# A planner's allowance for late operands of the tensor engine, applied only behind the in-projection

## Chip, cores and metric

The kernel runs on one core of a Trainium2 chip. The metric is the device time of one execution in microseconds (us). Engines are named as in the profile: PE is the tensor engine, DVE the vector engine, ACT the scalar engine, POOL GpSimd, and SP SyncE, which here issues every DMA.

## What is computed

One decoder layer on 1024 tokens of width 1024, all in float32. Two head groups, eight heads each, read one normed input through one input projection; their outputs go through one output projection, and a SwiGLU feed-forward part follows.

```python
xn = rms_norm(x, norm1_g)
proj = xn @ w_in                                  # 1024 x 3328
q, k, v, p_rw = split(proj, [512, 1024, 1536])
attn = rms_norm(dilated_attention(q, k, v))       # three dilated windows, ALiBi
rwkv = rwkv7_time_mix(p_rw, ...)                  # a scan over the tokens, 64 x 64 state per head
x = x + concat([attn, rwkv]) @ w_out
xn2 = rms_norm(x, norm2_g)
out = x + (silu(xn2 @ w_gate) * (xn2 @ w_up)) @ w_down
```

## The kernel before

Every wide product is made of three matmuls on operands split into a high and a low part: one block of 1024 x 128 weights takes 24 matmuls of 512 columns for each half of the tokens. The program has four stretches.

1. The in-projection (`inproj`, weights from `fetches` and `load_in`, results taken by `feed`): 26 blocks of 128 columns in `blocks`, the recurrence's first, then q, k and v. Each block is done for both halves of the tokens.
2. The recurrence (`decays`, `keys`, `scoring`, `sides`, `turn`, `invert`, `merge`, `chain`, `post`) runs beside it. There are eight units (four pairs of heads, two halves of the tokens) of eight steps each; 64 steps must follow one another. `chain` is the sequential part; each step goes back and forth between PE and the copying engines:

```python
yield PE.matmul(out=X[:, 0:128], lhsT=ra[:, c, :], rhs=Sc, ...)          # "S,ra"
for o in halves:
    yield DVE.tensor_copy(R[o, o], X[64:128, o])
yield PE.matmul(out=X[:, 128:256], lhsT=M[:, 1, c, :], rhs=R, ...)       # "Rb,M"
yield DVE.tensor_copy(vs[64:128, :], X[64:128, 128:256])
for o in halves:
    yield ACT.activation(Uc[o, o], X[64:128, 128 + o.start:128 + o.stop], AF.Copy)
yield PE.matmul(out=X[:, 256:384], lhsT=kbT[:, c, :], rhs=vs, ...)       # "VS,kbT"
yield PE.matmul(out=X[:, 0:128], lhsT=M[:, 1, c, :], rhs=Uc, ...)        # "Ub,M"
for e in range(2):
    yield DVE.scalar_tensor_tensor(out=Sn[o, o], ...)                    # state of the next step
```

   `post` norms a unit's output and stores it to `mix_d`.
3. Attention (`attn_load`, `value_load`, `attend` with `near` and `far`, `finish`) and the output projection (`fetch_wo`, `load_wo`, `mix_load`, `mix_T`, `outproj`, `add_up`). Attention's pool `pa` is opened when the in-projection is through; the output projection's pool lies where the recurrence's tiles were, and its streams are added when the recurrence is through.
4. The feed-forward part (`fetch_ff`, `prepare_ff`, `ffproj`, `gates`, `hidden`, `weight_sums`, `down`, `finals`).

The order of the instructions on each engine is not written out. Each part is a generator, a stream, that yields operations, waits for marks and requests for banks of PSUM. `Flow.run` keeps a clock for each engine and takes, again and again, the stream whose next operation can start first by its own costs (`scan`), by rank among those that are ready. `Flow.ready` gives the time at which an operation can start: for an operand that another engine wrote, the end of that operation plus that engine's `LAG`. For an operation of PE it adds another 60 ns and `LATE`, 300 ns. So a matmul is placed no earlier than that, and others, those of the in-projection above all, are placed ahead of it. These times only set the order; on the chip each engine runs its instructions in that order, and semaphores make it wait for real.

`flow.run` is called in turn for `dense` (the in-projection and `feed`), `rwkv` (the recurrence), `attn`, `ph3` (output projection and second norm) and the feed-forward part. All instructions are issued from one line, L235 (`emit`), so the profile's groups are told apart by their tiles: `mm`, `bank` and `chain` are banks of PSUM, `inhi` and `inlo` a block of in-projection weights, `xn0..` and `xn1..` the normed input, `kk`, `qv`, `vv` keys, queries and values of attention, `sb` its scores, `woraw`, `woh` and `wol` weights of the output projection.

Of the kernel before, what the change touches and what calls it, by code (L numbers as in the profile page):

```python
# [47 lines left out]
LAG = {"PE": 200, "ACT": 145, "DVE": 140, "POOL": 65, "SP": 1500}  # L48


LATE, SWITCH = 300, 100
# [7 lines left out]
class Op:  # L59


    def __init__(self, eng, name, fn, a, k):
        self.eng, self.name, self.fn, self.a, self.k = eng, name, fn, a, k
# [40 lines left out]
class Flow:  # L104
# [2 lines left out]


    def __init__(self):
        self.now, self.clk, self.marks, self.streams = 0.0, {}, {}, []  # L110
        self.slots, self.keys, self.count, self.shared = {}, {}, {}, set()
        self.free, self.weights, self.whole = {}, 0.0, True
# [67 lines left out]
    def ready(self, s):  # L180
        op = s.head
        if isinstance(op, Wait):
            if any(m not in self.marks for m in op.marks):
                return None
            return max((self.marks[m] for m in op.marks), default=0.0)
        if isinstance(op, Get):
            t, n = sorted(self.free[op.kind].values()), op.n or 1
            return t[n - 1] if len(t) >= n else None
        r = self.clk.get(op.eng, 0.0)
        if op.eng == "SP":  # L190
            r = max(r, self.clk.get("queues", 0.0) - 3000)
        for keys, which in ((op.rd, 0), (op.wr, 0), (op.wr, 1)):
            for k in keys:
                if k in self.slots:
                    for e, t in self.slots[k][which].items():
                        if e != op.eng or (e == "SP" and (keys is op.rd or which)):
                            r = max(r, t + LAG[e] + (60 + LATE if op.eng == "PE" else 0))
                        elif keys is op.rd and which == 0:
                            r = max(r, t + OWN[e])
        return r  # L200
# [67 lines left out]
def hymba_kernel(ctx: ExitStack, tc: tile.TileContext, x, w_in, w2a2, g2, w_out, w_gate, w_up,  # L268
# [3 lines left out]
    flow = Flow()  # L272
    ACT, DVE, POOL = Lane("ACT", nc.scalar), Lane("DVE", nc.vector), Lane("POOL", nc.gpsimd)
    PE, SP = Lane("PE", nc.tensor), Lane("SP", nc.sync)
# [1073 lines left out]


    flow.run(dense)  # L1350
    pw.__exit__(None, None, None)
    p1.__exit__(None, None, None)
    flow.free["bank"].update(mm0=flow.now, mm1=flow.now)
# [617 lines left out]
```

## Time and profile before

| what | us |
|---|---|
| median of 3 runs (lowest to highest) | 1462.24 (1461.12 to 1463.45) |
| the profiled execution's own time | 1464.17 |
| its span, first to last instruction | 1462.4 |
| PE busy in the span | 1389.5 (95%), 8578 records |
| weight loads of PE | 1123.4 (77%) |
| DVE busy | 899.8 (62%) |
| ACT busy | 726.3 (50%) |
| POOL busy | 701.4 (48%) |

The profile page gives busy time by engine, and one digit of busy share for each fortieth of the span. A matmul of float32 in two passes leaves two records. Matmuls are pipelined and their ends are modelled, so records overlap: the distance from one start to the next is the price of a matmul, not its duration. The views used below are the busy time in chosen stretches, the timeline of single engines, the list of waits, and the chain of work that ended last. In a timeline a row is a start, a duration, the engine, the operation and its tiles (written, then read), the shape, how many equal instructions it merges, and in brackets the idle time before it with what ended it.

### The profile page before, as it was taken

The page shows a single profiled execution, that of the slowest core. Times are in us where ns is not written, and L with a number is a line of the kernel's source. Part 1 is how long each engine was busy: PE and PEld are TensorE (multiplying, and loading weights), DVE is VectorE, ACT ScalarE, POOL GpSimd, SP SyncE. Part 2 cuts the span into 40 slices and gives each one's busy share as a digit, 9 for nine tenths or more (in the row PEclk, how much of TensorE's full clock was granted, in tenths as well). Part 3 has the DMA queues.
Part 4 walks back from the last instruction along what each step waited for, and adds up shares of the span by engine and source line. Part 5 has one row for each costly group of instructions (what it writes and reads, how often), then busy time and mean ns, then how long its engine had stood idle before and what let it go on. Part 6 is the DMA issues. An engine that isn't in the chain of part 4 may idle for free. (4 is left out here: it accounts for less than half of the span.)

```text
span 1462.4 us, 24926 instructions
## 1 busy us (share of the span) xinstructions
PE 1389.5 (95%) x8578; PEld 1123.4 (77%) x8578; DVE 899.8 (62%) x1812; ACT 726.3 (50%) x1794; POOL 701.4 (48%) x685
## 2 busy tenths in 40 slices
PE   7999989999999996699999899999999999999998
PEld 5777767777777885588878678888888888888887
DVE  5556677657576436667876855555555555666655
ACT  6434456566766776556764623333333333444443
POOL 4443344345565461433353845555555555644443
PEclk9999999999999998799999899999999999999999
DMA  5343222323333336699722235444444445865765
GB/s 193 115 119 72 68 80 83 94 75 110 93 110 109 110 127 175 186 280 235 198 76 75 72 115 165 151 148 146 154 151 165 153 165 181 280 200 188 225 221 173
DMA packets 217794, 213.45 MB, mean 146 GB/s; under 512 B 41026, under 2 KB 152898, under 8 KB 217667
## 3 DMA queue, kind: packets, MB, share of 16 engines
q1 hardware_dynamic: 217666, 211.85, 47.3%
q8 instruction: 68, 1.11, 0.3%
q14 instruction: 60, 0.48, 0.1%
HBM read 148.61 MB, written 58.98 MB: 142 GB/s over the span
## 5 line engine op out<-in xcount | busy, mean ns | idle before, releaser
L235 POOL TENSOR_TENSOR opl<-fraw,oph 128x512 fp32r<-128x512 f32 x79 | 110.8, 1405 | 180.7 <-PE bank L235 46.6
L235 POOL TENSOR_TENSOR opl<-raw,oph 128x512 fp32r<-128x512 f32 x74 | 97.1, 1312 | 99.9 <-ACT oph L235 95.6
L235 DVE TENSOR_TENSOR opl<-raw,oph 128x512 fp32r<-128x512 f32 x74 | 102.0, 1381 | 68.5 <-ACT oph L235 68.4
L235 ACT ACTIVATE oph<-raw 128x512 fp32r<-128x512 f32 x148 | 85.5, 624 | 114.3 <-PE mm L235 62.9
L235 ACT ACTIVATE oph<-sw 128x512 fp32r<-128x512 f32 x80 | 50.6, 633 | 180.4 <-PE chain L235 53.3
L235 POOL TENSOR_TENSOR inlo<-inraw,inhi 128x512 fp32r<-128x512 f32 x62 | 82.0, 1323 | 85.2 <-ACT inhi L235 72.7
L235 ACT ACTIVATE oph<-fraw 128x512 fp32r<-128x512 f32 x82 | 51.2, 627 | 76.7 <-PE bank L235 32.4
L235 DVE TENSOR_TENSOR opl<-sw,oph 128x512 fp32r<-128x512 f32 x80 | 75.8, 947 | 19.6 <-ACT oph L235 18.3
L235 PE MATMUL bank<-oph 128*128 128x512 f32 x154 | 59.9, 389 | 0.0
L235 PE MATMUL bank<-opl,oph 128*128 128x512 f32 x154 | 59.9, 389 | 0.0
L235 PE MATMUL bank<-oph,opl 128*128 128x512 f32 x154 | 59.9, 389 | 0.0
L235 DVE TENSOR_TENSOR uu<-bank,uu 128x512 f32<-128x512 f32 x20 | 13.9, 693 | 73.1 <-PE bank L235 73.1
L235 DVE SCALAR_TENSOR_TENSOR S<-chain,ec,Sp 64x64 f32<-64x64 f32 x112 | 31.6, 282 | 42.2 <-PE chain L235 35.5
L235 ACT ACTIVATE Ub<-chain 64x64 f32<-64x64 f32 x128 | 28.1, 219 | 54.2 <-DVE VS L235 51.9
L235 POOL TENSOR_TENSOR sw<-fraw 128x512 f32<-128x512 f32 x40 | 51.9, 1298 | 0.0
L235 ACT ACTIVATE Y<-chain 64x64 f32<-64x64 f32 x128 | 26.8, 211 | 49.0 <-DVE S L235 43.7
L235 ACT ACTIVATE inhi<-inraw 128x512 fp32r<-128x512 f32 x62 | 38.7, 624 | 16.0 <-PE mm L235 6.5
L235 DVE COPY Rb<-chain 64x64 f32<-64x64 f32 x128 | 28.9, 226 | 27.9 <-PE chain L235 25.5
L235 ACT ACTIVATE sb<-sb,mx 128x256 f32<-128x256 f32 (+3 forms) x64 | 36.2, 567 | 16.9 <-DVE mx L235 16.8
L235 POOL TENSOR_TENSOR rsf<-smf,nhalf 128x8 f32<-128x8 f32 x16 | 26.6, 1660 | 30.3 <-DVE smf L235 23.2
L235 DVE COPY VS<-chain 64x128 f32<-64x128 f32 x64 | 18.9, 295 | 31.6 <-PE chain L235 30.4
L235 PE MATMUL bank<-ra,kb 64*64 64x128 f32 x512 | 37.4, 277 | 0.0
(509 smaller groups left out, 4362.6 us busy)
## 6 DMA issues: line engine op xcount, KB each, us to landing
inraw<-in_w_in_dram SPq DMA_DIRECT2D x62, 256.0 KB, 3.0
fraw<-in_w_gate_dram SPq DMA_DIRECT2D x48, 256.0 KB, 3.8
fraw<-in_w_up_dram SPq DMA_DIRECT2D x48, 256.0 KB, 3.0
ws<-in_w_down_dram SPq DMA_DIRECT2D x22, 512.0 KB, 5.7
t_d<-ws SPq DMA_DIRECT2D x44, 256.0 KB, 3.0
raw<-s_d SPq DMA_DIRECT2D x44, 256.0 KB, 2.7
raw<-t_d SPq DMA_DIRECT2D x44, 256.0 KB, 3.1
s_d<-first SPq DMA_DIRECT2D x33, 256.0 KB, 4.1
```

What stands on the lines that cost most here:

```text
L235: op.fn(*op.a, **op.k)
```

## The change

The fixed `LATE` in `Flow.ready` becomes a field of the planner. It is 0 at first and is set to `LATE` when `flow.run(dense)` returns, that is when the planner has issued everything of the in-projection and of `feed`. Nothing else is changed; `LATE` stays 300.

```diff
     def __init__(self):
+        self.late = 0.0
         self.now, self.clk, self.marks, self.streams = 0.0, {}, {}, []
...
                     for e, t in self.slots[k][which].items():
                         if e != op.eng or (e == "SP" and (keys is op.rd or which)):
-                            r = max(r, t + LAG[e] + (60 + LATE if op.eng == "PE" else 0))
+                            r = max(r, t + LAG[e] + (60 + self.late if op.eng == "PE" else 0))
...
     flow.run(dense)
+    flow.late = LATE
     pw.__exit__(None, None, None)
```

Every engine's order changes from its first tens of instructions on. Three places follow. The first is on PE, one early step of the recurrence (the one that begins at 192.0 us in the profile), before:

```order
L235 MATMUL chain_2021<-S_118,ra 128x128
L235 MATMUL mm_2066<-xn10l,inhi 128x512 x3
L235 MATMUL mm_2066<-xn10h,inlo 128x512 x4
L235 MATMUL chain_2021<-Rb_124,M 128x128
L235 MATMUL chain_2119<-Vb_122,M 128x128
L235 MATMUL mm_2029<-xn1h_96,inhi 128x512 x2
L235 MATMUL mm_2029<-xn1h_97,inhi 128x512 x2
L235 MATMUL mm_2029<-xn1l_98,inhi 128x512 x2
L235 MATMUL mm_2029<-xn1l_99,inhi 128x512 x2
L235 MATMUL chain_2021<-VS,kbT 128x128
L235 MATMUL chain_2021<-Ub_126,M 128x128
```

The same step now:

```order
L236 MATMUL chain_1964<-S_118,ra 128x128
L236 MATMUL mm_1867<-xn11l,inhi 128x512
L236 MATMUL mm_1867<-xn11h,inlo 128x512 x4
L236 MATMUL chain_1964<-Rb_124,M 128x128
L236 MATMUL chain_2056<-Vb_122,M 128x128
L236 MATMUL mm_2050<-xn0h,inhi 128x512 x4
L236 MATMUL mm_2050<-xn0l,inhi 128x512 x2
L236 MATMUL chain_1964<-VS,kbT 128x128
L236 MATMUL chain_1964<-Ub_126,M 128x128
```

Between S,ra and Rb stand five wide matmuls instead of seven, between Rb and VS six instead of eight.

The second place is on PE, the end of the in-projection (its last block is on bank mm), before:

```order
L235 MATMUL mm_6283<-xn11h,inlo 128x512
L235 MATMUL chain_6320<-VS,kbT 128x128
L235 MATMUL chain_6320<-Ub_125,M 128x128
L235 MATMUL mm_6283<-xn11h,inlo 128x512 x2
L235 MATMUL chain_6345<-S_120,ra 128x128
L235 MATMUL chain_6345<-Rb_124,M 128x128
L235 MATMUL chain_6393<-Vb_122,M 128x128
L235 MATMUL bank_6400<-cs,vf_6398 128x128 x4
L235 MATMUL chain_6345<-VS,kbT 128x128
```

And now:

```order
L236 MATMUL mm_6475<-xn11h,inhi 128x512 x4
L236 MATMUL chain_6427<-Ub_126,M 128x128
L236 MATMUL mm_6475<-xn11l,inhi 128x512 x4
L236 MATMUL mm_6475<-xn11h,inlo 128x512 x3
L236 MATMUL bank_6526<-cs,exf_6511 128x128 x4
L236 MATMUL mm_6475<-xn11h,inlo 128x512
L236 MATMUL bank_6555<-cs,vf_6553 128x128 x4
L236 MATMUL bank_6635<-kk,qv 128x128 x2
```

Before, seven steps of the recurrence (S,ra, Rb and Ub, with six each of VS and Vb) follow the last in-projection matmul; now the last matmul of the last step, Ub_126, stands ahead of the last eight wide ones, and attention's first matmul follows the last values' transposes.

The third place is on SP, ahead of the first load of the output projection's weights, before:

```order
L235 DMA qv_6675<-qh_d_71 64x512
L235 DMA qv_6675<-ql_d_72 64x512
L235 DMA bias_6676<-in_tab_dram 128x512
L235 DMA vv_6704<-v_d_76 128x4x128
L235 DMA vv_6745<-v_d_76 128x4x128
L235 DMA mix_d_77<-Y_6318 128x2x128
L235 DMA woraw_6843<-in_w_out_dram 128x512
```

And now:

```order
L236 DMA mix_d_77<-Y_5971 128x2x128
L236 DMA v_d_76<-v01_6562 128x2x256
L236 DMA v_d_76<-v11_6563 128x2x256
L236 DMA qv_6610<-qh_d_71 64x512
L236 DMA qv_6610<-ql_d_72 64x512
L236 DMA bias_6611<-in_tab_dram 128x512
L236 DMA kk_6624<-kh_d_73 64x512 x2
L236 DMA kk_6624<-kl_d_74 64x512 x2
L236 DMA qv_6629<-qh_d_71 64x512
L236 DMA qv_6629<-ql_d_72 64x512
L236 DMA bias_6630<-in_tab_dram 128x512
L236 DMA woraw_6607<-in_w_out_dram 128x512
```

Before, the weights' load stands behind the last store of the recurrence, which comes after four heads' loads; now that store stands ahead of the last stores of the values, and the weights follow after two heads.

## Rows read from the trace of the kernel before

**Rows 1.** Busy time by stretch: us, each engine's busy us (records), clock, DMA share, GB/s.

```profile
50.00:547.00 497.00, 476.63 (x4217) 376.24 (x4215) 303.00 (x742) 299.38 (x853) 230.56 (x234) 1.00 0.33 97
547.00:561.00 14.00, 7.85 (x37) 6.28 (x35) 5.42 (x15) 8.12 (x30) 5.84 (x6) 0.68 0.56 172
561.00:596.00 35.00, 22.44 (x144) 18.08 (x143) 25.39 (x86) 18.91 (x68) 4.30 (x4) 0.98 0.44 121
596.00:623.00 27.00, 20.10 (x94) 16.06 (x95) 17.76 (x63) 17.47 (x49) 14.10 (x12) 0.70 0.95 267
623.00:761.00 138.00, 131.39 (x874) 113.78 (x873) 103.17 (x366) 93.58 (x301) 52.33 (x93) 0.99 0.76 199
761.00:802.00 41.00, 41.00 (x208) 33.98 (x207) 26.99 (x49) 19.23 (x36) 16.51 (x27) 1.00 0.30 91
842.00:1462.00 620.00, 615.44 (x2688) 503.94 (x2686) 358.74 (x411) 217.42 (x364) 326.40 (x245) 1.00 0.54 176
```

**Rows 2.** Timeline of PE, the end of the in-projection.

```profile
545.67 0.71 PE L235 MATMUL mm<-xn11h,inlo 128*128 128x512 f32 x2
546.68 0.49 PE L235 MATMUL chain<-S,ra 128*128 128x128 f32 x2 [0.29 <-DVE S L235]
...
560.49 1.84 PE L235 MATMUL bank<-kk,qv 128*128 128x128 f32 x6
```

**Rows 3.** Timeline of SP's queue, 551 to 597 us.

```profile
551.96 1.93 SPq L235 DMA_DIRECT2D v_d<-v  x2
553.98 0.45 SPq L235 DMA_DIRECT2D qv<-qh_d  x1
...
558.15 0.59 SPq L235 DMA_DIRECT2D qv<-qh_d  x1
...
595.74 0.36 SPq L235 DMA_DIRECT2D mix_d<-Y  x1
596.19 2.34 SPq L235 DMA_DIRECT2D woraw<-in_w_out_dram  x5
```

**Rows 4.** Waits of PE, 50 to 547 us: total us, times, longest.

```profile
PE chain L235 <- ACT Ub L235: 5.3, 9, 1.0
PE chain L235 <- DVE S L235: 5.1, 7, 1.8
...
PE chain L235 <- DVE Rb L235: 2.0, 5, 0.6
```

**Rows 5.** Timeline, one step of the recurrence, 419 to 424 us.

```profile
419.57 0.38 PE L235 MATMUL chain<-S,ra 128*128 128x128 f32 x2
...
419.99 0.47 DVE L235 COPY Rb<-chain 64x64 f32<-64x64 f32 x2 [0.99 <-PE chain L235]
...
420.95 0.38 PE L235 MATMUL chain<-Rb,M 128*128 128x128 f32 x2
...
421.70 0.45 ACT L235 ACTIVATE Ub<-chain 64x64 f32<-64x64 f32 x2 [0.79 <-DVE VS L235]
...
422.77 0.38 PE L235 MATMUL chain<-VS,kbT 128*128 128x128 f32 x2
...
422.99 0.39 PE L235 MATMUL chain<-Ub,M 128*128 128x128 f32 x2
```

**Rows 6.** The chain that ended last: start, us, twelve wide matmuls.

```profile
887.26 2.79 PE chain L235 x12
```

**Rows 7.** Timeline, another step of the recurrence, 196 to 198 us.

```profile
196.38 0.22 ACT L235 ACTIVATE Ub<-chain 64x64 f32<-64x64 f32 x1
...
197.22 0.49 PE L235 MATMUL chain<-VS,kbT 128*128 128x128 f32 x2 [0.85 <-ACT Ub L235]
```

**Rows 8.** Busy time from 561 to 596 us on the tiles kk, vv and sb.

```profile
561.00:596.00 35.00, 7.33 (x31) 4.86 (x30) 0.98 0.44 121
...
561.00:596.00 35.00, 6.40 (x32) 4.06 (x32) 0.98 0.44 121
...
561.00:596.00 35.00, 6.00 (x37) 4.33 (x37) 5.45 (x12) 8.57 (x25) 0.98 0.44 121
```

## Prediction

> **What bounds the kernel now.** I read the busy time by stretch first. Up to 547 us the tensor engine (PE) is busy in 476.6 of 497 us, from 623 to 802 in 172.4 of 179, and in the feed-forward part, 842 to the end, in 615.4 of 620 [rows 1]. Between 547 and 623 it is busy in only 50.4 of 76 us, and its granted clock means 0.68 and 0.70 in two of those three stretches [rows 1]. So PE work is the bound nearly everywhere, and the loose time lies behind the in-projection.
>
> The timeline says why. The last in-projection matmul starts at 545.67; behind it the recurrence still turns, with waits, and the first attention matmul comes at 560.49 [rows 2]. By the order of the instructions seven of the 60 steps with a state (those that begin with S,ra) are left then. They alternate PE, DVE and ACT, and nothing wide enough stands between. SyncE shows the other price: the last store of the recurrence (mix_d) goes out at 595.74, and the first load of the output projection's weights (woraw) only at 596.19, right behind it [rows 3].
>
> Inside the in-projection PE waits little for the recurrence: 5.3 + 5.1 + 2.0 = 12.4 us in 9 + 7 + 5 = 21 waits, out of some 165 hand-overs of these three kinds [rows 4]. There the 300 ns of allowance shows as slack: in a step that nothing hinders, the two Rb copies end at 419.99 + 0.47 = 420.46 and their matmul starts at 420.95; the Ub copies end at 421.70 + 0.45 = 422.15 and the next chain matmul starts at 422.77 [rows 5]. That is about half a microsecond to spare each time.
>
> **The change part by part.** No operation is added or removed, only the order is planned anew, with operands of PE assumed 300 ns earlier until the in-projection is through.
>
> *Work that moves.* In the new order all 64 steps stand ahead of the last in-projection matmul. 37 matmuls of 128 columns in two passes (7 each of S,ra, Rb and Ub, 6 each of VS and Vb, 4 of the gates) move from behind it to ahead of it, at 0.22 each (422.77 to 422.99 [rows 5]): 8.1 us.
>
> *Shorter cover.* Counted over the two orders at 0.23 for 512 columns (2.79 us for 12 [rows 6]) and 0.11 a record of 128 columns (half of the 0.22), the PE work between S,ra and Rb falls from a mean of 1.52 to 1.30 us, from Rb to VS from 2.28 to 1.88, from Ub to the next S,ra from 2.18 to 2.11: cuts of 0.22, 0.40 and 0.07, 0.69 a step. An unhindered step has the spare time for this [rows 5] and pays nothing. A step in which an engine's queue is late pays the whole cut: at 196.38 ACT only begins a Ub copy, and VS waits 0.85 at 197.22 [rows 7]. The 21 waits of today grow by 9 x 0.40 + 7 x 0.07 + 5 x 0.22 = 5.2 us. I take twice that, 10 us, for the hand-overs that just miss a wait today and for the others (square sums, head norms) that lose their 300 ns too. Bounds: 0, if a longer wait at one place only gives the other engines time to catch up, and 64 x 0.69 = 44, if nothing covers anything; 10 lies near the low end because the unhindered step does. So the in-projection ends at 545.67 + 0.71 + 8.1 + 10 = 564.5.
>
> *The pause.* From that end to the first load of queries (qv) pass 553.98 - 546.38 = 7.6 us [rows 2, 3]: the last values are turned, split and stored (551.96) first. This chain is not touched, and I keep 7.6; what leaves it is the recurrence, so that PE stands idle there instead. It costs nothing by itself, since before too no attention could run.
>
> *The loads.* On SyncE mix_d now stands ahead of those stores, and woraw follows after two heads' loads: ten issues. Seven took 4.17 us (553.98 to 558.15 [rows 3]), so ten take 6. Woraw goes out at 564.5 + 7.6 + 6 = 578.0 instead of 596.19: 18.2 us earlier.
>
> *Attention done before that.* What attention had done by 596 has still to be done: 31 + 32 + 37 = 100 records on the tiles kk, vv and sb [rows 8]. At the 0.11 of the smallest they are 11 us, by their busy times 7.33 + 6.40 + 6.00 = 19.7, which overlap. I take 14, nearer the low end for that overlap. From the weights' request to the end I leave the 866 us as they are: in 623 to 802 PE is all but full, and the feed-forward part is the same work.
>
> Sum: -18.2 + 14 = -4.2 us against the profiled execution's 1464.17, so 1460.0 there. It lies 1.9 above the median of the runs shown, 1462.24; against that the forecast is **1458.0 us**. A difference of 0.2%, 2.9 us, is about what a measurement can tell from none.
>
> [...] After 552 PE has no wide matmuls left, and the granted clock means 0.68 from 547 to 561; after the stall near 590 it means 0.70 from 596 to 623 [rows 1]. [...]
>
> **The rivals.**
> 1. *A larger gain.* Today attention starts with six banks and four score buffers while the recurrence holds DVE; in the new order it has eight of each from the start and the output projection at hand as filler. If the ramp of 596 to 623 goes at the pace of 623 to 761 (95% busy, clock 0.99), it gives back 27 - 20.1/0.95 = 5.8 us, and with waits of 5 instead of 10 us another 5: 1447. For it speaks the unhindered step; against it the DMA engines, 95% busy there [rows 1].
> 2. *Slower: the waits take more than the tail gives.* The place is the in-order DVE and ACT queues, where inversions, keys and norms stand ahead of the Rb and Ub copies [rows 7]; each late copy now stops the in-projection matmuls queued behind its consumer. It decides from 10 + 4.2 = 14.2 us of added waits. At half of the 44, 22 us: 1458.0 + 12 = 1470. For it speaks that Rb to VS, with the most waits, is cut most.
> 3. *No change: the clock and the loads.* If the pause and then the ramp both run at the low clock, the 20.1 us busy of 596 to 623, some 60% of it at half speed, come a second time in part: 20.1 x 0.6 x 0.5 = 6 us at most, I take 5: 1463.
>
> That the recurrence still ends late cannot be: PE keeps its order, and the last step stands ahead of the last in-projection matmul.
>
> **How the numbers follow.** Forecast 0.40 (within 6 us, so 0.32 faster and 0.08 same), larger gain 0.17, slower 0.25, no change 0.18 (0.02 faster, 0.12 same, 0.04 slower). Faster by over 0.2% is 0.51, within it 0.20, slower 0.29. The range reaches from 1446, the larger gain and a little beyond (11 instead of 14 us of attention gives 3 more), to 1471, the slower case; the rest of the bound of 44 us is left out.
>
> **What would show it.** Right: no chain matmul behind the last in-projection matmul; that one ends at 560 to 570; PE's waits for Ub, S and Rb in that stretch sum to 20 to 25 instead of 12.4 us; then some 13 us with PE nearly idle; woraw goes out near 578. Wrong: an in-projection that ends behind 570, or attention that from its first matmul on takes longer than today by more than the 14 us of the term above.

## The result and the profile after

The changed kernel takes 1481.35 us, median of 4 runs (1474.32 to 1483.55); the kernel before, on the same chip, 1462.85 (1461.12 to 1464.41). The ratio is **1.0114, 95% interval 1.0094 to 1.0134** (the quotient of the two medians alone is 1.0126); by the medians it is 18.5 us slower, where 4 us less were forecast. It lies outside the range. A comparison leaves out executions more than 1.5% above the fastest of their kernel; the medians beside it count all.

The profiled execution took 1483.0 us, its span 1481.2 at a mean granted clock of 0.973; before, 1464.17, 1462.4 and 0.982. The busy time by stretch, to be read against [rows 1]:

```profile
0.00:50.00 50.00, 41.02 (x172) 26.99 (x173) 24.80 (x45) 27.11 (x50) 19.59 (x42) 0.81 0.48 161
157.00:164.00 7.00, 6.46 (x85) 5.28 (x84) 5.39 (x12) 2.16 (x7) 2.50 (x3) 0.52 0.14 41
164.00:262.00 98.00, 92.81 (x822) 70.30 (x820) 68.81 (x172) 57.76 (x194) 38.50 (x43) 1.00 0.26 74
262.00:284.00 22.00, 20.41 (x259) 14.04 (x245) 11.04 (x24) 8.38 (x26) 6.03 (x9) 0.69 0.27 77
500.00:581.00 81.00, 78.13 (x439) 65.08 (x437) 38.57 (x100) 57.15 (x163) 45.83 (x39) 1.00 0.38 119
581.00:593.00 12.00, 2.82 (x12) 2.41 (x12) 4.72 (x12) 2.83 (x6) 2.25 (x2) 0.62 0.58 188
593.00:610.00 17.00, 10.64 (x53) 8.88 (x52) 10.01 (x34) 10.85 (x28) 3.80 (x3) 0.66 1.00 290
610.00:630.00 20.00, 16.44 (x96) 14.08 (x95) 11.15 (x41) 11.13 (x32) 1.27 (x2) 0.83 0.99 267
630.00:770.00 140.00, 128.35 (x878) 110.42 (x876) 106.50 (x392) 97.28 (x316) 56.39 (x95) 0.99 0.76 196
862.00:1481.00 619.00, 614.29 (x2684) 503.04 (x2682) 358.06 (x411) 217.28 (x364) 325.98 (x244) 1.00 0.54 176
```

Three of these stretches in the kernel before:

```profile
0.00:50.00 50.00, 40.64 (x187) 28.31 (x188) 26.20 (x45) 28.23 (x53) 20.83 (x44) 0.90 0.50 167
157.00:164.00 7.00, 7.00 (x92) 5.56 (x91) 6.23 (x13) 3.92 (x11) 1.23 (x1) 1.00 0.11 40
262.00:284.00 22.00, 21.43 (x179) 16.59 (x173) 14.12 (x40) 13.54 (x39) 7.85 (x11) 1.00 0.42 113
```

The column behind POOL is the granted clock. The feed-forward part is the same. Ahead of it two things are new: the clock is low in 157 to 164 and 262 to 284 us, where PE is over 92% busy, and at the start; and 630 to 770, the bulk of attention, is busy in 128.35 of 140 us (92%), not 131.39 of 138.

The end of the in-projection on PE, in the changed kernel; [rows 2] before:

```profile
580.37 0.48 PE L236 MATMUL mm<-xn11h,inlo 128*128 128x512 f32 x1
583.10 0.66 PE L236 MATMUL bank<-cs,vf 128*128 128x128 f32 x4 [2.26 <-ACT vf L236]
590.84 2.69 PE L236 MATMUL bank<-kk,qv 128*128 128x128 f32 x8 [7.08 <-issue]
594.90 1.08 PE L236 MATMUL mm<-kk,qv 128*128 128x128 f32 x3 [1.37 <-DMA qv<-qh_d]
...
601.42 1.09 PE L236 MATMUL bank<-cs,mixr 128*128 128x128 f32 x4 [3.84 <-DMA mixr<-mix_d]
```

SyncE's queue there; [rows 3] before:

```profile
585.48 0.37 SPq L236 DMA_DIRECT2D mix_d<-Y  x1
585.94 1.10 SPq L236 DMA_DIRECT2D v_d<-v  x2
587.14 0.47 SPq L236 DMA_DIRECT2D qv<-qh_d  x1
...
593.28 2.27 SPq L236 DMA_DIRECT2D woraw<-in_w_out_dram  x5
```

PE's waits for the recurrence, 50 to 581 us (total us, times, longest); [rows 4] before:

```profile
PE chain L236 <- DVE Rb L236: 7.8, 12, 1.7
PE chain L236 <- ACT Ub L236: 7.6, 10, 1.8
...
PE chain L236 <- DVE S L236: 0.9, 2, 0.4
```

The order did what was said: no recurrence matmul follows the in-projection, PE is nearly idle from 581 to 593, and the weights follow 12.4 us behind the in-projection's end (580.85). But that end came 34.5 us later than the 546.38 of before, so the weights went out only 2.9 us earlier (593.28 for 596.19); and from there to the end it took 887.9 us, not 866.2. 2.9 against 21.7: 18.8 us longer, the difference of the two spans.

**Where the time went.** PE issues the same work in every kernel here, so each execution can be split. For each matmul I took the distance to the next start and subtracted its own price at full clock (0.23 for 512 columns, 0.22 for 128 in two passes, and so on). Of what is left, low clock (the granted clock is 0.50 there) takes at most half of the time at low clock in that gap; the remainder is a wait where the next matmul has an operand from another engine or a DMA, and "rest" where it has none. A split by such prices is an estimate; its "rest" shows how far it can be trusted, some 3 us.

| PE, us | in-projection's end | work | waits | clock | rest | behind it: work | waits | clock | rest | span |
|---|---|---|---|---|---|---|---|---|---|---|
| before | 546.0 | 491.8 | 49.1 | 4.9 | -1.3 | 831.7 | 50.5 | 20.3 | 9.6 | 1462.4 |
| changed | 580.4 | 500.0 | 56.2 | 20.5 | 2.2 | 823.6 | 44.9 | 18.6 | 9.5 | 1481.2 |
| changed, another execution | 571.4 | 500.0 | 60.7 | 6.6 | 2.6 | 823.6 | 41.9 | 21.8 | 9.1 | 1472.0 |
| 0 for the chain alone | 566.9 | 497.3 | 57.3 | 7.8 | 3.0 | 826.2 | 40.4 | 22.1 | 8.2 | 1468.1 |
| 0 for all but the chain | 561.8 | 491.4 | 57.3 | 11.7 | 0.0 | 832.2 | 48.6 | 25.1 | 9.6 | 1481.9 |
| 300, from turn 6 on 0 | 565.5 | 499.5 | 58.1 | 3.5 | 3.0 | 824.0 | 41.2 | 23.4 | 9.0 | 1467.5 |
| 0, from turn 6 on 300 | 550.4 | 491.8 | 49.3 | 9.9 | -2.1 | 831.7 | 46.6 | 20.2 | 9.5 | 1462.6 |
| 150 | 565.8 | 498.4 | 53.6 | 11.1 | 1.3 | 825.1 | 37.4 | 17.4 | 9.0 | 1459.3 |

(The end is the start of the last in-projection matmul; work, waits, clock and rest count from the first matmul on.) In the profiled execution the in-projection's 34.4 us are 8.2 of moved work, 7.1 of waits, 15.6 of clock, 3.5 unresolved. The rest is higher in every kernel in which most of the seven steps move (1.3 to 3.0 for -1.3), so a part of it may be a cost of the new orders that the split can't name. Behind it the moved work comes off in full (8.1), but waits fall by only 5.6.

### The profile page after: what moved, and what is told of

It is laid out like the page before. It is cut to its first block, busy times and chain, and to the rows that moved or that the text cites. A ratio compares the mean times of both kernels' runs of the same rounds, so it can differ in the third digit from the quotient of the medians.

```text
span 1481.2 us, 24951 instructions
## 1 busy us (share of the span) xinstructions
PE 1402.2 (95%) x8578; PEld 1127.3 (76%) x8578; DVE 900.4 (61%) x1812; ACT 722.0 (49%) x1794; POOL 700.1 (47%) x685
## 5 line engine op out<-in xcount | busy, mean ns | idle before, releaser
L236 DVE TENSOR_TENSOR up<-bank,uu 128x512 f32<-128x512 f32 x40 | 27.6, 689 | 18.3 <-PE bank L236 18.3
L236 PE MATMUL bank<-kk,qv 128*128 128x128 f32 (+3 forms) x128 | 27.3, 329 | 11.8 <-issue 7.1
```

The lines of the kernel that those rows point to most:

```text
L236: op.fn(*op.a, **op.k)
```

## The experiments

Two theories stood first. **Clock**: work other than the recurrence's chain has lost its allowance too, PE stops more often at the start and among narrow matmuls, and its clock falls (0.81 in the first 50 us for 0.90 before, 0.52 at 157 to 164, 0.69 at 262 to 284). That the stops bring the falls was assumed. **Waits**: the chain's cut cover stops PE, rival 2 of the prediction.

**1. The chain alone without the allowance**

```diff
-    ... (60 + self.late if op.eng == "PE" else 0)
+    ... (60 + (self.late if s.rank == 3 else LATE) if op.eng == "PE" else 0)
```

> The allowance is 0 in the in-projection for the sequential recurrence (chain) alone; everything else keeps 300 ns. Two steps stay behind the in-projection by the order. Theory CLOCK (15.6 of the 34 us by which the in-projection ends later are the low clock, which comes where narrow matmuls of scoring, merge and the start lose their allowance): low clock between 50 us and the end of the in-projection at most 7 us instead of 20.5, the in-projection ends at 553 to 565, time 1455 to 1468. Theory WAITS (the chain's own hand-overs cost it): waits of PE for Ub, S and Rb stay at 16 us or more, the end at 570 or later, time 1473 or more.

1466.46 us, ratio 1.0022 (1.0006 to 1.0038). The chain's zero alone moves 5.5 us of work ahead of the in-projection's end, costs 8.2 of waits and 2.9 of clock there (with 4.3 unresolved), and takes 10.1 of waits off behind it. The time is in CLOCK's range; the end of the in-projection (566.9) is 2 us behind CLOCK's, and PE's waits for Ub, S and Rb sum to 20.9 us, as WAITS had it, without the loss that it saw in them. The chain alone carries two thirds of the moved work and a small part of the loss.

**2. All but the chain without it**

```diff
+    ... (60 + (LATE if s.rank == 3 else self.late) if op.eng == "PE" else 0)
```

> The other half: in the in-projection the chain keeps 300 ns, everything else has 0. Seven steps stay behind the in-projection as before. CLOCK: low clock inside the in-projection of 7 us or more and a slow start of 57 instead of 52.5 us; since nothing is gained behind it, time 1468 to 1478. WAITS: within 4 us of before, 1459 to 1467, and no low clock between 50 us and the end of the in-projection.

1480.21 us, ratio 1.0119 (1.0093 to 1.0145). Seven steps stay behind, nothing is gained, and the in-projection still ends 15.8 us later: 8.2 of waits and 6.8 of clock. Chain 0.2%, the rest 1.2%: that speaks for the clock theory, though the time is 2 us above its range. But the clock of this profile is 0.81 in the first 50 us and 0.99 from 50 to 564. The first takes some 9.5 of the 11.7 us of clock in the table, (1 - 0.81) x 50; the other 2.2 are some 4 to 5 us at low clock, an estimate, where the theory asked for 7 or more. And the split shows as many added waits here as in experiment 1. So the theory had only half of it: either half of the change costs waits, and this half buys nothing with them.

**3. 150 ns instead of 0**

```diff
-        self.late = 0.0
+        self.late = 150.0
```

> 150 ns instead of 0 in the in-projection. One step stays behind it. CLOCK: all or nothing, since a low clock comes or does not come: with none inside the in-projection 1460 to 1466, with one stretch of 7 to 14 us up to 1472. WAITS: half of the loss, near 1472, with the full clock throughout.

1461.02 us, ratio 0.998 (0.9958 to 1.0002). The time is in CLOCK's range, but not for its reason: ahead of the in-projection's end the clock costs 11.1 us, more than before. There half of the allowance adds 4.5 us of waits (53.6 for 49.1; none of it left, 7.1 and 11.6), one step is left behind, and the in-projection ends no earlier than in experiment 4 below. What makes this kernel as fast as the one before lies behind that: 37.4 us of waits for 50.5, and 17.4 of clock for 20.3.

**4. 300 at the start, 0 from the seventh turn of the in-projection's weights on**

```diff
-        self.late = 0.0
+        self.late = LATE
...
         for n, (u, hs) in enumerate(turns[1:], 1):
+            if n == 6:
+                flow.late = 0.0
```

> 300 ns until the seventh turn of the in-projection, 0 from there to its end: the start is as before. CLOCK: the start of 52.5 us comes back and with it 5 us (5.2 us of low clock), the low clock of 20 us inside the in-projection stays: 1472 to 1479. WAITS: the start did not matter, within 3 us of the changed kernel, 1478 to 1484.

1467.72 us, ratio 1.0037 (1.0021 to 1.0054). Its order on PE equals that of before up to 70 us. The in-projection's last matmul starts at 565.5, and so it ends (565.9) 1.4 us behind the forecast, with work +7.7, waits +9.0, clock -1.4. The weights go out when the prediction said, at 578.0:

```profile
577.77 2.33 SPq L236 DMA_DIRECT2D woraw<-in_w_out_dram  x5
```

From there to the end it takes 1467.5 - 577.77 = 889.7 us, where the forecast had 880. So the forecast up to the weights' request was about right where the clock stays up (it is 1.00 from 50 to 566 us; the later end and a pause that was 1.8 us shorter than forecast cancel), and the kernel is slower all the same: the miss of this run lies behind the request.

**5. The opposite: 0 at the start, 300 behind it**

> The allowance is 0 from the start of the kernel to the turn n == 6 of the in-projection and 300 ns from there on: the opposite of the run that kept 300 ns there. If the order of the start costs only there, the changed kernel's extra low clock and waits of the first 50 us return (start 56 to 57 us in place of 52.5, low clock around 20 us), the in-projection keeps its 492 us, and the kernel takes 1467 to 1470 us. If the 18.5 us of the changed kernel came from the mere order inside the in-projection, the start alone is worth nothing and the time is within 2 us of the kernel before.

1464.08 us, ratio 1.0006 (0.9988 to 1.0025). The in-projection ends 4.4 us later, by the clock (9.9 for 4.9), and waits behind it give 3.9 back (46.6 for 50.5). The start alone is worth less than 2 us, as the second expectation had it.

**6. 300 at the start, then 150**

> 300 ns to the turn n == 6, then 150 ns to the end of the in-projection. By the theory of the clock the start keeps its 50 to 52.5 us and the in-projection loses no more than 3 us of clock, so the kernel takes 1456 to 1463 us. By the theory of waits the waits lie between those at 300 and those at 0 (40 and 50 us) and the time between those kernels', 1463 to 1468 us.

1475.05 us, ratio 1.0086 (1.0053 to 1.0119). Both expectations missed. Its weights go out only at 599.0, four steps are left behind, and waits behind the in-projection are 47.3. Two edits that each helped by themselves do not add up.

**7. The changed kernel once more**

> The changed kernel once more, for another profiled execution. If the low clock comes from the order of the work, it is found in the same places again (at 14, at 41, near 157 and near 270 us) with 30 us or more before the end of the in-projection, and the time is 1474 to 1484 us. If the stretches at 157 and 270 us were a chance of that execution, the clock before the in-projection's end is full outside the start and the profiled execution is some 10 us shorter.

1475.66 us, ratio 1.0084 (1.0056 to 1.0112). The stretches of the profile above, in this execution:

```profile
0.00:50.00 50.00, 40.35 (x184) 26.88 (x185) 24.78 (x45) 28.49 (x53) 20.89 (x44) 0.90 0.50 166
157.00:164.00 7.00, 7.00 (x37) 5.58 (x37) 6.70 (x16) 2.10 (x9) 0.00 (x0) 1.00 0.13 36
262.00:284.00 22.00, 19.35 (x214) 13.98 (x212) 17.65 (x44) 10.91 (x31) 7.21 (x11) 1.00 0.38 104
```

The clock is full at both places, and the start is like that of before. These rows are of the same times and not of the same matmuls (x37 here, x85 there), so the whole stretch says more:

```profile
50.00:547.00 497.00, 470.40 (x4166) 366.61 (x4164) 304.78 (x757) 292.66 (x871) 225.81 (x231) 1.00 0.32 93
```

The same program had 14 us less of clock cost ahead of the in-projection's end, and the median stays 13 us above that of before. So the low stretches belong to an execution, and the slowdown does not hang on them alone.

**8. The output projection ranked ahead of attention's later work**, on top of experiment 4

```diff
-            flow.add(7.8, add_up()), flow.add(9.5, outproj())]
+            flow.add(7.8, add_up()), flow.add(8.1, outproj())]
```

> The kernel with 300 ns to the turn n == 6 and 0 behind it, and the out-projection ranked ahead of the attention's later work (9.5 becomes 8.1), so that 96 instead of 187 of its 384 matmuls stand behind the last attention matmul. If the remainder from the loads' request to the end was longer than forecast because out-projection work was left for the time behind the attention, the gap from the last attention matmul to the last out-projection matmul falls from 55 to 30 us or less and the kernel takes 1455 to 1463 us. If the out-projection only fills time that the attention would wait in anyway, the attention grows by what the tail loses and the time stays at 1466 to 1470 us.

1505.75 us, ratio 1.0291 (1.0266 to 1.0317), a miss of both. The gap behind the last attention matmul does fall to 35 us, but attention grows by 53 us over experiment 4: from the in-projection's end on 59.3 of waits for 41.2 and 39.2 of clock for 23.4. The output projection's matmuls had filled attention's waits; done early, they are missing later, and the clock is low for longer (the time at low clock, worked out as further below, is 91.8 us on average in 4 executions, 50.7 in 10 of experiment 4). That more of them are left behind attention in the changed kernel (187 for 160 of 384) is therefore no loss that this rank gives back.

**9. The recurrence's output loaded ahead of the weights**, on top of experiment 4

```diff
-... flow.add(7.5, mix_load()), ...
+... flow.add(3.7, mix_load()), ...
```

> The kernel with 300 ns to the turn n == 6 and 0 behind it, with one rank changed: the loads of the recurrence's output (mixr) go out ahead of the output projection's weights instead of behind five of them. In the run without this the tensor engine stood 3.63 us for mixr right behind the in-projection. If that wait is the part of the ramp that my 14 us left out, it falls to 1 us or less, the stretch from the first weights' request to the end shrinks by 3 us and the kernel takes 1463 to 1466 us in place of 1467.7. If another operand (the weights, or keys and queries) is late next, the wait only changes its name and the time stays at 1467 to 1469 us.

1468.51 us, ratio 1.0046 (1.0032 to 1.006). PE's two longest waits behind the in-projection (565 to 650 us) in experiment 4, without the edit:

```profile
PE bank L236 <- DMA kk<-kh_d: 6.6, 1, 6.6
PE bank L236 <- DMA mixr<-mix_d: 3.6, 1, 3.6
```

And with it:

```profile
PE bank L236 <- DMA bias<-in_tab_dram: 5.9, 1, 5.9
PE chain L236 <- DMA qv<-ql_d: 3.2, 1, 3.2
```

The wait for mixr is down to 0.3, and PE stands for queries and for attention's table instead. The wait only changed its name, as the second expectation had it.

**10. The same on top of the 150 ns** (the candidate to beat both)

> 150 ns up to the end of the in-projection, with the same change of the rank of the mixr loads: the candidate for a kernel that beats both. If the mixr wait counts, 1457 to 1460 us, under the 1461.0 without it; if another operand is late next, 1460 to 1463 us.

1461.61 us, ratio 0.9999 (0.9983 to 1.0015): no gain over 150 ns alone (0.998), as the second expectation had it.

**11 and 12. 200 and 100 ns**

> 200 ns up to the end of the in-projection, four steps of the recurrence behind it. If the time follows the allowance smoothly, it lies between those at 150 and 300 ns, 1460 to 1463 us. If every order is a draw of its own (where the steps end, where the clock falls, what the attention's start waits for), it may lie anywhere from 1458 to 1478 us.

> 100 ns up to the end of the in-projection, two steps behind it. If the time follows the allowance smoothly, it lies between those at 150 and at 0 ns, near 1466 us. If every order is a draw of its own, it may lie anywhere from 1458 to 1478 us, and under 1461 or over 1472 us shows it.

200 ns: 1459.87 us, ratio 0.9991 (0.9965 to 1.0017). 100 ns: 1468.29 us, ratio 1.0044 (1.0023 to 1.0065). With the 1462.3 of before at 300, 1461.0 at 150 and 1477.7 at 0 (median of the 9 runs of the two comparisons), the time is flat from 300 down to 150 and rises below. This is the smooth expectation; experiment 6 is the exception to it.

**13. The weights' loads spread behind the attention's operands**, on top of experiment 4

```diff
-    ph3 = [flow.add(3.8, fetch_wo()), ...
+    ph3 = [flow.add(7.65, fetch_wo()), ...
```

> The kernel with 300 ns to the turn n == 6 and 0 behind it, with the loads of the output projection's weights ranked behind those of mixr and of the values (3.8 becomes 7.65): three weights' loads instead of five, and behind the mixr and three vv loads, follow the first two heads. If the waits of the attention's start come from five weights' loads that stand ahead of its operands on the queue, the waits from the end of the in-projection to the end fall by 5 us or more below the 41.2 us of the run without this, and the kernel takes 1460 to 1464 us. If the start is bound by the operands' total transfer, in whatever order they go out, the waits stay within 3 us and the time stays at 1466 to 1470 us.

1467.62 us, ratio 1.0043 (1.0027 to 1.006); 42.1 us of waits behind the in-projection for 41.2 without it. The longest ones now:

```profile
PE bank L236 <- DMA bias<-in_tab_dram: 6.0, 1, 6.0
PE chain L236 <- DMA woraw<-in_w_out_dram: 4.8, 1, 4.8
```

Again another operand is the late one. With experiment 9 this says that neither of these two orders on the queue takes the waits away; that the transfers' total is the cause was not shown.

**14. 200 ns once more**

> 200 ns up to the end of the in-projection once more. The first profiled execution took 1483 us with low clock for 24 us from 208 us on, while the median was 1459.9. If the fall is a chance of one execution, this profile has none there, ends some 20 us earlier with the same waits, and the median is 1458 to 1462 us. If it belongs to the order, it returns at 208 us.

1461.01 us, ratio 1.0013 (0.9986 to 1.004). Busy time from 200 to 240 us in the first execution of the 200 ns kernel:

```profile
200.00:240.00 40.00, 37.82 (x292) 27.42 (x292) 22.46 (x47) 16.14 (x49) 11.10 (x12) 0.70 0.23 64
```

And in this one:

```profile
200.00:240.00 40.00, 38.03 (x401) 28.16 (x401) 28.77 (x71) 19.12 (x62) 13.45 (x15) 0.98 0.32 85
```

One program, spans of 1481.2 and 1455.1 us. Of the 26.1 us between them 17.1 are clock ahead of the in-projection's end (22.1 for 5.0), by the split above. The fall is a chance of one execution.

**No version beat both kernels, the one before and the changed one.** 150 and 200 ns cannot be told from the kernel before.

## Why the prediction was wrong

*What held.* The moved work: 8.1 us forecast, 8.2 by the split. The added waits: 10 forecast, 7.1 and 11.6 in the changed kernel's two profiles, 9.0 in experiment 4. They did not come where they were put: PE's waits for Ub, S and Rb sum to 16.3 us in one profile and 16.2 in the other, not to 20 to 25. Rb, whose cut was 0.22, took the most (7.8 for 2.0); Ub, with the largest cut, took less (7.6 for 5.3), and S lost its waits (0.9 for 5.1). The rest of the added waits is at other hand-overs, for which the prediction had only doubled its sum. That the total came near 10 is in part luck. The pause to the first query load: 7.6 forecast, 587.14 - 580.85 = 6.3. The ten issues: 6, measured 593.28 - 587.14 = 6.1. So up to the weights' request the terms of the sum held in size; what came on top was the clock, and some 3.5 us that the split leaves unresolved.

*First failed step: the in-projection's cost was priced without the clock.* "So the in-projection ends at 545.67 + 0.71 + 8.1 + 10 = 564.5" had no term for it, since the granted clock of before is 1.00 from 50 to 547 [rows 1]. In the profiled execution it was 15.6 us (a third of that in the start, the rest at 157 to 164 and 262 to 284), in the next one 1.7. Because it varies so, it is better read over all executions. In windows of 1 us the granted clock is 1.00 in 1405 of 1462 in the profile before and in 1391 of 1481 in the changed kernel's, 0.50 in 41 and in 72; each of the others holds a change between the two. So time at low clock is (1 - mean granted clock) x span / 0.5. Half of it is counted as lost, an estimate from four wide matmuls that take 1.71 us to the next start at 280.50 in the changed kernel's profile, and 0.92 at 70.75, at full clock. The time at low clock has a mean of 54.9 us in 91 executions of the kernel before, 67.9 (41 to 83) in 9 of the changed one. That is (67.9 - 54.9) / 2 = **6.5 us** of the slowdown, which is 15 us by the means of these executions. With nine executions it is uncertain by about 5 us: the first four alone give 11, the next five 3. In the 27 executions of experiments 4, 9 and 13 it was 50.1, less than before, so the extra clock cost is not a must of planning without the allowance; which part of the order raises its chance stays open. The start alone (experiment 5, 56.5) did not show it, nor did the chain alone (experiment 1, 51.0 in 10); all but the chain did (experiment 2, 65.1), in four executions only.

*Second failed step: "From the weights' request on I leave the 866 us as they are".* With the 14 us of attention work I had 880; it took 887.9 in the changed kernel, 887.7 in its second profile and 889.7 in experiment 4, where the weights had gone out as forecast. By the split the work that had still to be done was 10.8 us, so the 14 was no underestimate of work; the waits are the rest, 37.7 us for 27.0 before (34.3 in the second profile); in experiment 4 a part of it is clock (23.4 us behind the in-projection for 20.3). They are thin and spread: in the changed kernel 3.0 more in the first 40 us, 4.6 in attention behind that, 2.1 in the rest of the output projection. My reason, "in 623 to 802 PE is all but full", was no proof that it stays so. My reading is that attention's waits for its own loads, scores and copies used to run partly beside the recurrence's last seven steps, and that they stayed when these left. Forecast from the in-projection's end to the end of the kernel: 22.3 us less; measured 15.7 less (1462.4 - 546.38 to 1481.2 - 580.85), and 15.8 in the second profile. 8.1 of it is the work, so 7.6 came from waits and clock, not 14.2. That the missing gain is this cover is argued from the split and stays open. It is borne out by one thing: with one step left (experiment 3) the in-projection ends as in experiment 4, but the waits behind it are 37.4 us, fewer than in any kernel of the table with none left (41.2 to 44.9). The one other rank of the output projection (experiment 8) and the two other orders of the loads (9, 13) did not bring the gain back.

*The sum without the clock.* Span less half of the low-clock time is 1433.2 on average before and 1441.7 in the changed kernel: 8.5 us slower with the clock out of it. The step "-18.2 + 14 = -4.2" falls even so: about 25 us are paid ahead of the end of the in-projection in the second profile (8.2 work, 11.6 waits, 1.7 clock, 3.9 unresolved), and 15.8 come back.

*The rivals.* The larger gain needed the ramp at full pace; 593 to 610 has a clock of 0.66 and DMA engines that are busy all the time (a share of 1.00). The slower rival had the sign, but not the size of its mechanism: 22 us of waits by its price, 7 to 12 by measurement, and its place was right only for Rb and Ub. The third, a ramp slower by the clock, fell: behind the in-projection the clock costs 18.6 us in the changed kernel, 21.8 in the second profile, 20.3 before. The half speed that it reckoned with is in the traces: us by us, the clock is 0.50 from 597 to 610 before and from 584 to 604 in the changed kernel. That an emptier pause makes the matmuls behind it slower was not shown: the clock means 0.62 and 0.66 from 581 to 610, but it added nothing, because the old order had its low stretches there too, 0.68 and 0.70 [rows 1]. The falls at 157 to 164 and 262 to 284 us came behind short stops (0.99 us, for V, and 1.39, for P) and not behind a pause. No run here shows that the stops caused them: in another execution of the same program (experiment 7) the longest waits for V and P were 0.9 and 1.4 us, and the clock was 1.00 in both stretches.

Of the two signs of being wrong, the first came: the in-projection ends at 580.85 and 571.83, behind 570. The second, as it was worded, did not. From its first matmul to its last on its own keys and values attention takes 769.6 - 590.8 = 178.8 us, where it took 759.2 - 560.5 = 198.7. What grew by more than the 14 us is the time from the weights' request to the end, by 21.7, and that was the term to watch.

## What to carry to other kernels

An allowance that looks like slack in an undisturbed step pays for the disturbed ones (7.1 and 11.6 us of added waits without it). Here a third or half of it could go at no cost that these runs can tell, all of it could not; try steps between before removing it. When work moves out of a stretch where two parts ran side by side, allow for the waits of the part that stays, not only for its work. And the same stop can stand ahead of a fall of the clock in one execution and of none in the next (1.39 us, and a clock of 0.69 in the 22 us around it; 1.40 us, and 1.00), so read the clock over all executions before a single profile is explained.

## What was not expected of the hardware

The granted clock fell in stretches in which PE was busy 92 to 93% of the time and no wait was longer than 1.39 us. (A matmul at low clock lasts longer, as the 1.91 us for 1.08 below show, so such a share stands for less work than the same share at full clock.) PE's timeline around the second fall of the changed kernel's profile, and a row at full clock from ahead of both:

```profile
70.75 1.08 PE L236 MATMUL mm<-xn11h,inlo 128*128 128x512 f32 x4
...
268.72 1.00 PE L236 MATMUL bank<-W,P 32*32 32x32 f32 x58 [1.39 <-DVE P L236]
269.92 0.80 PE L236 MATMUL chain<-Rb,M 128*128 128x128 f32 x2 [0.20 <-DVE Rb L236]
...
278.92 1.06 PE L236 MATMUL bank<-u1t,M 32*32 32x32 f32 x32
279.91 0.80 PE L236 MATMUL mm<-xn1h,inlo 128*128 128x512 f32 x1
280.50 1.91 PE L236 MATMUL mm<-xn11h,inhi 128*128 128x512 f32 x4
```

Four wide matmuls that take 1.08 at full clock take 1.91 at 280.50. What PE did before were many matmuls of 32 x 32 with short stops between them. But this alone did not make it fall. The same 58 matmuls behind the same stop, and the two of 64 x 512 that follow, in the second execution of the same program, where the clock stayed full:

```profile
264.38 1.00 PE L236 MATMUL bank<-W,P 32*32 32x32 f32 x58 [1.40 <-DVE P L236]
...
266.42 1.12 PE L236 MATMUL bank<-wa,w2a2s 64*128 64x512 f32 x2
```

In the first execution these two took 2.07, at low clock:

```profile
271.33 2.07 PE L236 MATMUL bank<-wa,w2a2s 64*128 64x512 f32 x2
```

The busy share does not tell a low stretch from a full one: 37.82 of 40 us at a clock of 0.70, 38.03 of 40 at 0.98, with 292 and 401 records (experiment 14). And the low-clock time of one program, the changed kernel, varied from 41 to 83 us between executions; half of the 42 us between them, 21 us, is more than the 18.5 that were to be explained.
